# Norm tiles, engine orders, norm statistics and the score sign in a two-layer decoder

## The chip, the cores and the metric

The kernel runs on one core of a Trainium2 chip. The metric is the time of one execution in microseconds (us), as the device measures it; lower is better. The kernel before took 2627.57 us (median of three runs, 2625.74 to 2631.69). Five engines work side by side: TensorE (PE in the profile, its weight loads PEld), VectorE (DVE), ScalarE (ACT), GpSimd (POOL) and SyncE (SP), whose queue starts the transfers.

## The reference, cut to what matters

The input is one sequence of 1024 positions by 1024 channels, in float32. Layer 0 is a causal convolution module and a gated FFN; then one set of keys and values is projected; layer 1 is sparse attention (compressed, selected and window branches, 16 heads) and a second FFN; a last RMSNorm ends it.

```python
def rmsnorm(x, g):
    return x * lax.rsqrt(jnp.mean(x * x, axis=-1, keepdims=True) + EPS) * g

def conformer_conv(x, ...):
    a, b = jnp.split(rmsnorm(x, norm_g) @ pw1_w + pw1_b, 2, axis=-1)
    h = depthwise_conv31(a * sigmoid(b)) + dw_b
    h = silu(layernorm(h, ln_g, ln_b))          # the channel norm
    return h @ pw2_w + pw2_b

h = x + conformer_conv(x, ...)
h = h + swiglu_ffn(h, ...)                      # rmsnorm, 1024 -> 2 x 2816 -> 1024
kv = shared_kv(h, ...)                          # rmsnorm (kv_norm), projection
h = h + nsa_attention(h, ...)                   # rmsnorm (b_norm), 16 heads, softmax(s - slope * dist)
h = h + swiglu_ffn(h, ...)
out = rmsnorm(h, final_norm)
```

## The kernel before, in words

Everything is held with channels on the partitions: a half of the sequence (512 positions, c = 0 or 1) is eight tiles of 128 x 512, k = 0 to 7. A float32 product is made of three TensorE matmuls on a high and a low part: `split` (L172) writes the high part yh on ScalarE (L177) and then the low part yl = y - yh on VectorE or GpSimd (L179); `wload` (L142) does the same for a weight tile (wh L158, wl L160), and `mm3` (L123, L137) issues wh*yh, wh*yl and wl*yh for each k. One weight tile against eight k is 24 matmuls.

A norm has these steps. `sumsq` (L182) squares a tile on ScalarE (L189) and adds it to an accumulator on VectorE or GpSimd (L190). `rstd_parts` (L192) makes the sum over channels: four small matmuls (L201), each with 128 columns of the accumulator as the stationary operand and one column of ones. They are put into a list, `sides`, and `mm3` issues one of them behind each of its own matmuls. Ten small VectorE operations make the reciprocal root (`rsqrt`, L252 to L262), a VectorE operation lays it on a diagonal (`diagonal`, L213), and a matmul with ones spreads it over the partitions (`spread`, L220). Then `norm_y` (L265) writes each normed tile (L272, VectorE) and splits it. While `roomy` holds (the first 760 us or so), every normed tile whose low part is made on VectorE is put into PSUM, in a pool of eight buffers with one tag that also serves all matmul results and the convolution; otherwise it goes into a temporary in SBUF (tag "a", five buffers, four later). In the channel norm, `centre` (L378) sums the accumulator over channels (L382), subtracts the mean (L385) and squares; `normal` (L393) multiplies by the reciprocal root (L401), applies SiLU on ScalarE (L403; for c = 0 into PSUM) and splits.

The norms, by the order in which their tiles are used: n1 and n2, the first RMSNorm of the halves 0 and 1; n3, the channel norm of half 0; n4, the FFN norm of half 0; n5, the channel norm of half 1; n6, the key/value norm of half 0; n7, the FFN norm of half 1; n8, the key/value norm of half 1; n9 and n10, the second FFN norms of the halves 0 and 1; n11, the last norm of half 0. Behind n6 and n8 an attention norm uses the same reciprocal root, kept in SBUF (`kept`). n1, n2 and n4 to n11 use one accumulator; n3 hands its eight squares to the statistics one by one.

TensorE's order is the order in which the program issues its matmuls. `go(main, time)` runs generators of foreground work for a stated time of TensorE; `behind` interleaves a second generator at a rate: the convolution of a half (`conv`, `conv_tile`, L303: up to ten taps on ScalarE and GpSimd, L328 and L329, four on TensorE, L320, the rest on VectorE, L332), then `layernorm(1)` (L408), later the attention. The `yield` numbers in `layernorm` are the times that pass between its steps. The orders of VectorE, ScalarE and GpSimd are written by a planner from its own times of the operations; buffers are given out in that plan, too. `mark` remembers an instruction of an engine, and `later` adds an edge without a semaphore that puts an instruction behind the one marked.

In attention `scores` (L949) adds scaled scores and a distance term and takes the running maximum in one VectorE operation (L987), negates the maximum (L993, VectorE), and ScalarE takes the exponential with it as the bias (L995).

Of the kernel before, what the change touches and what calls it, by code (L numbers as in the profile page):

```python
# [20 lines left out]
F32 = mybir.dt.float32  # L21
# [6 lines left out]
KT = 8  # L28
NC = 2
T = 512  # L30
# [7 lines left out]
NEG = -1e30  # L38
# [60 lines left out]
PRINT = 0  # L99
YB = 16  # L100


class Net:
# [69 lines left out]
    def split(self, src, lo="dve"):  # L173
# [3 lines left out]
        nc.scalar.activation(yh, src, AF.Copy)  # L177
# [4 lines left out]
    def sumsq(self, c, k, src, eng, pool=None):  # L182
# [107 lines left out]


# [102 lines left out]
    def normal(self, c):  # L394
# [4 lines left out]
        y = []  # L399
        for j in range(KT):  # L400
            self.later(nc.vector.tensor_tensor(z[j], z[j], r, OP.mult))  # L401
            s = self.tmp("si") if c or j in LNP[c] else self.mm_ps()
            nc.scalar.activation(s, z[j], AF.Silu, bias=self.vec[:, V_LNB + j:V_LNB + j + 1],  # L403
                                 scale=self.vec[:, V_LNG + j:V_LNG + j + 1])
            y.append(self.split(s, "pool" if j in LNP[c] else "dve"))
        if c == 0:
            self.mark(self.last)
        self.yln[c] = y  # L408

    def layernorm(self, c):  # L410

        yield 4.0
        self.centre(c)
        yield 10.0
        self.sides.extend(self.rstd_parts([self.acc[c]]))
        yield 6.0
        while self.sides:
            yield 1.0
        self.rstd_spread(c, True)
# [408 lines left out]
    def q_tile(self, j, c):  # L828
# [73 lines left out]
    def bias_base(self):  # L902
# [3 lines left out]
        for (c0, w, step, off) in ((0, S, 1, 896), (BT_WIN, 640, 1, 512),  # L906
                                   (BT_CMP, 119, 16, 896 - (LC - 1))):
            nc.gpsimd.iota(b[:, c0:c0 + w], pattern=[[step, w]], base=-off,
                           channel_multiplier=-1, allow_small_or_imprecise_dtypes=True)
            nc.gpsimd.affine_select(out=b[:, c0:c0 + w], in_=b[:, c0:c0 + w],  # L910
                                    pattern=[[-step, w]], compare_op=OP.is_ge, fill=NEG,
                                    base=off, channel_multiplier=1)
        nc.gpsimd.affine_select(out=b[:, BT_WIN:BT_WIN + 640], in_=b[:, BT_WIN:BT_WIN + 640],
                                pattern=[[1, 640]], compare_op=OP.is_ge, fill=NEG,
# [34 lines left out]
    def scores(self, out, K, q, g, head, i, win):  # L949


        nc = self.nc
# [589 lines left out]
```

## Time and profile before

| | |
|---|---|
| median of three runs | 2627.57 us (2625.74 to 2631.69) |
| the profiled execution | 2629.18 us |
| its span, first to last instruction | 2627.5 us |
| PE busy | 2512.0 us, 96% |
| DVE busy | 1765.8 us, 67% |
| POOL busy | 1469.2 us, 56% |
| ACT busy | 1291.6 us, 49% |
| mean granted TensorE clock | 0.981 |

A share is an average over stages with different limits. An engine's idle time costs something only where the instruction that it waits for ends last, so the waits of TensorE are what is to be read, each at its place in the timeline. The granted clock is a share of full speed: 1.00 is 2.4 GHz, 0.50 is 1.2 GHz.

### The profile page before, as it was taken

What the parts mean: (1) busy time and instruction counts of PE and PEld (TensorE: products, weight loads), DVE (VectorE), ACT (ScalarE), POOL (GpSimd) and SP (SyncE); (2) the same over time, 40 slices, a digit from 0 to 9 for tenths busy, and PEclk for the clock granted to TensorE, in tenths of its full rate; (3) what the DMA queues carried; (4) which work ended last, traced back from release to release, by engine and by line L of the source; (5) the groups of instructions that cost most, each with busy time, mean ns of one, the idle gap of its engine ahead of it and who ended that gap; (6) DMA issues with size and microseconds to landing.
All of it is one profiled execution on the core that took longest, in us unless ns stands there. A gap on an engine that the chain in (4) does not pass through costs nothing. (4 is left out here: it accounts for less than half of the span.)

```text
span 2627.5 us, 37191 instructions
## 1 busy us (share of the span) xinstructions
PE 2512.0 (96%) x12946; PEld 2083.5 (79%) x12946; DVE 1765.8 (67%) x3652; ACT 1291.6 (49%) x2517; POOL 1469.2 (56%) x1156
## 2 busy tenths in 40 slices
PE   8898899999799999999999999999999999899997
PEld 6676788888677878887878788888888887698986
DVE  6995788677774556665556566667666655777775
ACT  6555554444534554555543355555555543334444
POOL 8794889666543554555543354535445433566664
PEclk9999899999899999999999999999999999999999
DMA  4222223232446222322355531213212124143332
GB/s 163 72 73 66 80 81 97 88 93 92 152 146 190 87 89 62 112 86 82 90 161 167 190 101 45 81 44 108 70 53 74 54 78 158 58 129 97 97 95 75
DMA packets 111212, 258.29 MB, mean 98 GB/s; under 512 B 17265, under 2 KB 28848, under 8 KB 111024
## 3 DMA queue, kind: packets, MB, share of 16 engines
q1 hardware_dynamic: 111024, 255.91, 31.0%
q8 instruction: 102, 1.67, 0.3%
q14 instruction: 86, 0.70, 0.1%
HBM read 226.37 MB, written 29.42 MB: 97 GB/s over the span
## 5 line engine op out<-in xcount | busy, mean ns | idle before, releaser
L160 POOL TENSOR_TENSOR wl<-wr,wh 128x1024 fp32r<-128x1024 f32 (+2 forms) x396 | 740.6, 1872 | 661.1 <-ACT wh L158 625.1
L137 PE MATMUL mm<-yh,wh 128*128 128x512 f32 x1424 | 595.4, 418 | 31.7 <-DVE yl L179 30.4
L137 PE MATMUL mm<-yl,wh 128*128 128x512 f32 x1424 | 567.6, 399 | 5.0 <-DVE yl L179 5.0
L137 PE MATMUL mm<-yh,wl 128*128 128x512 f32 x1424 | 566.2, 398 | 1.8 <-POOL wl L160 1.8
L158 ACT ACTIVATE wh<-wr 128x1024 fp32r<-128x1024 f32 (+2 forms) x396 | 332.5, 840 | 426.3 <-PE mm L137 287.1
L137 PE MATMUL mm<-gh,wh 128*128 128x512 f32 x1360 | 439.4, 404 | 1.8 <-ACT gh L592 1.4
L137 PEld LDWEIGHTS mm<-yh,wh 128*128 128x128 f32 x1424 | 272.1, 191 | 86.3 <-DVE yl L179 32.1
L137 PEld LDWEIGHTS mm<-yh,wl 128*128 128x128 f32 x1424 | 271.3, 191 | 63.5 <-POOL wl L160 2.2
L137 PEld LDWEIGHTS mm<-yl,wh 128*128 128x128 f32 x1424 | 272.6, 191 | 49.5 <-DVE yl L179 6.2
L1030 DVE TENSOR_TENSOR pl<-pt,ph 128x512 fp32r<-128x512 f32 (+3 forms) x320 | 206.4, 646 | 149.6 <-ACT ph L1029 148.7
L137 PEld LDWEIGHTS mm<-gh,wh 128*128 128x128 f32 x1360 | 243.3, 189 | 48.8 <-issue 3.5
L137 PE MATMUL mm<-gh,wl 128*128 128x512 f32 x680 | 270.0, 397 | 3.7 <-POOL wl L160 3.7
L1029 ACT ACTIVATE ph<-pt 128x512 fp32r<-128x512 f32 (+3 forms) x320 | 178.7, 559 | 177.6 <-PE pt L1026 175.2
L1000 POOL TENSOR_SCALAR PS<-PS,sm,gates 128x31 f32<-128x31 f32 (+9 forms) x256 | 154.7, 615 | 191.4 <-DVE sm L997 164.6
L332 DVE SCALAR_TENSOR_TENSOR mm<-u,vec,mm 128x512 f32<-128x512 f32 x306 | 225.6, 752 | 8.0 <-PE mm L320 1.8
L995 ACT ACTIVATE PS<-PS,mx 128x31 f32<-128x31 f32 (+9 forms) x256 | 139.5, 546 | 115.6 <-DVE mx L993 115.3
L329 POOL TENSOR_TENSOR zb<-zb,cv 128x512 f32<-128x512 f32 x132 | 178.8, 1355 | 14.4 <-ACT zb L314 8.8
L1000 POOL TENSOR_SCALAR PW<-PW,sm,gates 128x640 f32<-128x640 f32 (+4 forms) x128 | 96.2, 752 | 155.1 <-DVE sm L997 131.8
L606 DVE TENSOR_TENSOR h<-mm,h 128x512 f32<-128x512 f32 x184 | 124.7, 684 | 81.7 <-PE mm L137 81.3
L137 PEld LDWEIGHTS mm<-gh,wl 128*128 128x128 f32 x680 | 128.0, 188 | 37.7 <-POOL wl L160 7.5
L995 ACT ACTIVATE PW<-PW,mx 128x640 f32<-128x640 f32 (+4 forms) x128 | 88.8, 694 | 101.2 <-DVE mx L993 100.5
L507 PE MATMUL mm<-y,wh 128*128 128x256 f32 x1008 | 133.8, 286 | 2.3 <-DVE wh L492 1.9
(243 smaller groups left out, 4814.4 us busy)
## 6 DMA issues: line engine op xcount, KB each, us to landing
wr<-in_fin_dram SPq DMA_DIRECT2D x176, 512.0 KB, 3.3
wr<-in_fout_dram SPq DMA_DIRECT2D x128, 256.0 KB, 2.7
wr<-in_pw_dram SPq DMA_DIRECT2D x46, 512.0 KB, 3.3
wr<-in_fout_dram SPq DMA_DIRECT2D x64, 192.0 KB, 2.4
wr<-in_wq_dram SPq DMA_DIRECT2D x16, 512.0 KB, 4.0
qd<-q SPq DMA_DIRECT2D x32, 256.0 KB, 2.2
qt<-qd SPq DMA_DIRECT2D x32, 256.0 KB, 2.8
wr<-in_wo_dram SPq DMA_DIRECT2D x16, 512.0 KB, 3.7
```

The costliest lines, as they stand in the source:

```text
L137: nc.tensor.matmul(ps, x[:, a, :], y_, start=start and a + b == 0, stop=stop and a == n - 1 and b == 2)
L158: nc.scalar.activation(wh[:, :kt, :cols], wr[:, :kt, :cols], AF.Copy)
L160: e.tensor_tensor(wl[:, :kt, :cols], wr[:, :kt, :cols], wh[:, :kt, :cols].bitcast(F32), OP.subtract)
L329: nc.gpsimd.tensor_tensor(zb, zb, t, OP.add)
L332: later(nc.vector.scalar_tensor_tensor(ps, u[:, w:w + T], dw(w), ps, OP.mult, OP.add))
L507: nc.tensor.matmul(ps, u[:, a], v, start=a + b == 0, stop=a == n - 1 and b == 2)
L606: self.nc.vector.tensor_tensor(h, ps, h, OP.add)
L995: nc.scalar.activation(P[:, p0:p0 + pn], P[:, p0:p0 + pn], AF.Exp, bias=mx[:, e:e + 1], accum_out=sm[:, e:e + 1])
L1000: nc.gpsimd.tensor_scalar(P[:, p0:p0 + pn], P[:, p0:p0 + pn], sm[:, e:e + 1], self.gates[:, i, gt:gt + 1], OP.mult, OP.mult)
L1029: nc.scalar.activation(ph[:rows, :width], pt[:rows, :width], AF.Copy)
L1030: nc.vector.tensor_tensor(pl[:rows, :width], pt[:rows, :width], ph[:rows, :width].bitcast(F32), OP.subtract)
```

## The change

Six things are changed. (1) In `norm_y`, while `roomy` holds, only even tiles go into PSUM; odd ones go into SBUF temporaries. (2) Edges without a semaphore fix orders: in `norm_y`, tile k is written behind the second-last low part made on VectorE before it; in `normal`, VectorE's multiplication stands behind the third-last low part, and ScalarE's SiLU behind the second-last high part; the attention norm's tiles stand behind the last low part of the key/value norm; for half 0, ScalarE's part of the later convolution stands behind the channel norm's last high part. (3) The last square of a norm is not added to the accumulator: it goes to the statistics as a second tile, so there are eight small matmuls in the place of four. (4) That last square takes a buffer of tag "rs" (two buffers, shared with the diagonal and the kept reciprocal root). (5) `layernorm(1)` has other times between its steps. (6) The score's sign is turned: queries, distances and the mask value have the other sign, a running minimum takes the place of the maximum, the exponential has scale -1, and the negation is gone.

```diff
+AHEAD = 2
...
-        nc.scalar.activation(yh, src, AF.Copy)
+        self.first = nc.scalar.activation(yh, src, AF.Copy)
...
             nc.scalar.activation(self.acc[c], src, AF.Square)
-        else:
+        elif k < KT - 1:
             sq = pool.tile([128, T], F32, name="sq", tag="b") if pool else self.tmp("sq")
             nc.scalar.activation(sq, src, AF.Square)
             eng.tensor_tensor(self.acc[c], self.acc[c], sq, OP.add)
+        else:
+
+            sq = self.sq[c] = self.cp.tile([128, T], F32, name="sl", tag="rs", bufs=2)
+            nc.scalar.activation(sq, src, AF.Square)
...
-        self.sides.extend(self.rstd_parts(tiles or [self.acc[c]]))
+        self.sides.extend(self.rstd_parts(tiles or [self.acc[c], self.sq[c]]))
...
-        y = []
+        y, low = [], []
         for k in range(KT):
-            t = self.mm_ps() if self.roomy and k not in pool else self.tmp("yt")
-            nc.vector.scalar_tensor_tensor(t, self.h[c][k], self.vec[:, vcol + k:vcol + k + 1],
-                                           r, OP.mult, OP.mult)
+            t = self.mm_ps() if self.roomy and k % 2 == 0 and k not in pool else self.tmp("yt")
+            ins = nc.vector.scalar_tensor_tensor(
+                t, self.h[c][k], self.vec[:, vcol + k:vcol + k + 1], r, OP.mult, OP.mult)
+            if kept:
+                self.later(ins)
+            if len(low) >= AHEAD:
+                self.order(ins, low[-AHEAD])
             y.append(split(t, k) if split else self.split(t, "pool" if k in pool else "dve"))
+            if not split and k not in pool:
+                low.append(self.last)
...
+    def order(self, ins, old):
+
+        self.tc.add_manual_dep(ins.ins, old.ins.name, mybir.DependencyInfo(
+            mybir.DependencyClass.NoSync, mybir.DependencyReason.DATA))
...
-            self.later(nc.vector.tensor_tensor(z[j], z[j], r, OP.mult))
+            ins = nc.vector.tensor_tensor(z[j], z[j], r, OP.mult)
+            self.later(ins)
+            if len(low) > AHEAD:
+                self.order(ins, low[-1 - AHEAD])
             s = self.tmp("si") if c or j in LNP[c] else self.mm_ps()
...
+            if len(high) >= AHEAD:
+                self.order(ins, high[-AHEAD])
             y.append(self.split(s, "pool" if j in LNP[c] else "dve"))
+            high.append(self.first)
+            if j not in LNP[c]:
+                low.append(self.last)
         if c == 0:
             self.mark(self.last)
+            self.mark(self.first)
...
     def layernorm(self, c):
 
-        yield 4.0
+        yield 10.0
         self.centre(c)
-        yield 10.0
-        self.sides.extend(self.rstd_parts([self.acc[c]]))
-        yield 6.0
+        yield 16.0
+        self.sides.extend(self.rstd_parts([self.acc[c], self.sq[c]]))
+        yield 1.0
         while self.sides:
             yield 1.0
+        yield 14.0
         self.rstd_spread(c, True)
...
-            f = DH ** -0.5 / SLOPE[g * HG + j]
+            f = -DH ** -0.5 / SLOPE[g * HG + j]
...
-                    SLOPE[head], init, OP.add, OP.max, mx[:, col:col + 1])
+                    SLOPE[head], init, OP.add, OP.min, mx[:, col:col + 1])
...
-        nc.vector.tensor_scalar(mx[:, :ns], mx[:, :ns], -1.0, None, OP.mult)
         for e, (br, p0, pn, b0) in enumerate(segs):
-            nc.scalar.activation(P[:, p0:p0 + pn], P[:, p0:p0 + pn], AF.Exp,
+            nc.scalar.activation(P[:, p0:p0 + pn], P[:, p0:p0 + pn], AF.Exp, scale=-1.0,
...
         self.y[0] = self.norm_y(0, V_KVN)
+        self.mark(self.last)
...
         self.y[1] = self.norm_y(1, V_KVN)
+        self.mark(self.last)
```

## Rows read from the trace of the kernel before

**Rows 1.** The page's first part: busy time, share of the span, instructions.
```profile
PE 2512.0 (96%) x12946; PEld 2083.5 (79%) x12946; DVE 1765.8 (67%) x3652; ACT 1291.6 (49%) x2517; POOL 1469.2 (56%) x1156
```

**Rows 2.** Stretches round eight waits: length; busy PE, PEld, DVE, ACT, POOL; PEclk; DMA.
```profile
103.50:116.10 12.60, 6.18 (x16) 4.82 (x16) 12.60 (x20) 6.82 (x12) 11.92 (x8) 0.60 0.31 107
232.70:245.70 13.00, 2.77 (x8) 2.15 (x8) 7.28 (x13) 11.89 (x20) 11.29 (x9) 0.61 0.14 42
293.80:304.10 10.30, 7.43 (x23) 6.13 (x24) 6.84 (x13) 3.83 (x6) 7.95 (x4) 0.67 0.31 102
307.20:317.70 10.50, 5.24 (x13) 4.14 (x14) 10.50 (x17) 7.18 (x13) 7.43 (x6) 0.67 0.16 51
698.60:710.10 11.50, 6.55 (x19) 5.51 (x20) 7.78 (x17) 4.21 (x5) 7.22 (x3) 0.70 0.50 160
714.60:727.10 12.50, 4.01 (x10) 3.14 (x11) 12.50 (x20) 5.53 (x10) 2.35 (x1) 0.59 0.30 106
1376.20:1386.10 9.90, 7.22 (x22) 6.02 (x23) 5.45 (x13) 2.81 (x4) 7.21 (x3) 0.66 0.59 189
2242.90:2249.70 6.80, 3.41 (x8) 2.69 (x9) 6.53 (x8) 3.19 (x7) 2.35 (x1) 0.75 0.23 77
```

**Rows 3.** The busy ends of two of these stretches, TensorE alone: length, busy, PEclk.
```profile
109.90:116.10 6.20, 6.17 (x15) 0.50 0.01 3
...
296.60:304.10 7.50, 7.43 (x23) 0.54 0.43 140
```

**Rows 4.** Timeline of TensorE, small matmuls among large ones: start, length, instruction.
```profile
209.36 0.40 PE L137 MATMUL mm<-yh,wh 128*128 128x512 f32 x1
209.59 0.28 PE L201 MATMUL mm<-ones,sq 128*128 128x1 f32 x2
...
210.04 0.28 PE L201 MATMUL mm<-ones,sq 128*128 128x1 f32 x2
```

**Rows 5.** Timeline: last sum before n3's centre, and the centre's matmul.
```profile
196.65 0.68 DVE L343 TENSOR_TENSOR acc<-acc,z 128x512 f32<-128x512 f32 x1
...
201.66 1.02 PE L382 MATMUL mm<-acc,ones 128*128 128x512 f32 x2
```

**Rows 6.** Busy time in two convolution stretches, columns as in Rows 2.
```profile
100.00:200.00 100.00, 91.87 (x357) 68.44 (x356) 96.35 (x133) 54.92 (x88) 83.59 (x53) 0.95 0.23 75
...
400.00:470.00 70.00, 70.00 (x306) 57.05 (x305) 58.38 (x80) 35.73 (x52) 62.65 (x41) 1.00 0.32 100
```

**Rows 7.** Low parts on VectorE by source: shapes, count | busy us, mean ns | idle.
```profile
L179 DVE TENSOR_TENSOR yl<-yt,yh 128x512 fp32r<-128x512 f32 x30 | 32.3, 1109 | 0.1
...
L179 DVE TENSOR_TENSOR yl<-mm,yh 128x512 fp32r<-128x512 f32 x30 | 19.1, 681 | 5.7 <-ACT yh L177 5.7
```

**Rows 8.** Timeline of ScalarE in n3 and at the first weight behind it.
```profile
231.62 1.47 ACT L403 ACTIVATE mm<-z,vec 128x512 f32<-128x512 f32 x2
...
241.61 2.98 ACT L177 ACTIVATE yh<-mm 128x512 fp32r<-128x512 f32 x6
...
252.56 1.06 ACT L158 ACTIVATE wh<-wr 128x1024 fp32r<-128x1024 f32 x1 [7.97 <-PE mm L137]
```

**Rows 9.** Timeline of VectorE: last accumulator sums of n4 and n6.
```profile
293.80 2.82 DVE L190 TENSOR_TENSOR acc<-acc,sq 128x512 f32<-128x512 f32 x1 [2.18 <-POOL acc L190]
...
699.26 4.23 DVE L190 TENSOR_TENSOR acc<-acc,sq 128x512 f32<-128x512 f32 x3
```

**Rows 10.** Timeline: last sum before n5's centre, and the centre's matmul.
```profile
456.39 2.83 DVE L343 TENSOR_TENSOR acc<-acc,z 128x512 f32<-128x512 f32 x1
...
463.14 1.02 PE L382 MATMUL mm<-acc,ones 128*128 128x512 f32 x2
```

**Rows 11.** Timeline of VectorE in n6: tiles of the attention norm.
```profile
717.83 3.34 DVE L272 SCALAR_TENSOR_TENSOR yt<-h,vec,rs 128x512 f32<-128x512 f32 x4
```

**Rows 12.** The score's negation on VectorE: shapes, count | busy us, mean ns | idle.
```profile
L993 DVE TENSOR_SCALAR mx<-mx 128x1 f32<-128x1 f32 (+1 forms) x256 | 81.0, 319 | 3.5
```

**Rows 13.** Waits of TensorE in attention: us in total, times, longest.
```profile
PE po L1051 <- DVE pl L1030: 3.4, 9, 0.7
```

More of the change, by code (lines that the diff above doesn't have):

```diff
@@ L37 @@
 EPS = 1e-6
-NEG = -1e30
+FAR = 1e30
 LC = 32
@@ L398, in normal @@
         r = self.rs[c] if c else self.rp[c]
-        y = []
+        y, low, high = [], [], []
         for j in range(KT):
-            self.later(nc.vector.tensor_tensor(z[j], z[j], r, OP.mult))
+            ins = nc.vector.tensor_tensor(z[j], z[j], r, OP.mult)
+            self.later(ins)
+            if len(low) > AHEAD:
+                self.order(ins, low[-1 - AHEAD])
             s = self.tmp("si") if c or j in LNP[c] else self.mm_ps()
-            nc.scalar.activation(s, z[j], AF.Silu, bias=self.vec[:, V_LNB + j:V_LNB + j + 1],
-                                 scale=self.vec[:, V_LNG + j:V_LNG + j + 1])
+            ins = nc.scalar.activation(s, z[j], AF.Silu,
+                                       bias=self.vec[:, V_LNB + j:V_LNB + j + 1],
+                                       scale=self.vec[:, V_LNG + j:V_LNG + j + 1])
+            if len(high) >= AHEAD:
+                self.order(ins, high[-AHEAD])
             y.append(self.split(s, "pool" if j in LNP[c] else "dve"))
+            high.append(self.first)
+            if j not in LNP[c]:
+                low.append(self.last)
         if c == 0:
             self.mark(self.last)
+            self.mark(self.first)
         self.yln[c] = y
     def layernorm(self, c):
-        yield 4.0
+        yield 10.0
         self.centre(c)
-        yield 10.0
-        self.sides.extend(self.rstd_parts([self.acc[c]]))
-        yield 6.0
+        yield 16.0
+        self.sides.extend(self.rstd_parts([self.acc[c], self.sq[c]]))
+        yield 1.0
         while self.sides:
             yield 1.0
+        yield 14.0
         self.rstd_spread(c, True)
@@ L907, in bias_base @@
                                    (BT_CMP, 119, 16, 896 - (LC - 1))):
-            nc.gpsimd.iota(b[:, c0:c0 + w], pattern=[[step, w]], base=-off,
-                           channel_multiplier=-1, allow_small_or_imprecise_dtypes=True)
+            nc.gpsimd.iota(b[:, c0:c0 + w], pattern=[[-step, w]], base=off,
+                           channel_multiplier=1, allow_small_or_imprecise_dtypes=True)
             nc.gpsimd.affine_select(out=b[:, c0:c0 + w], in_=b[:, c0:c0 + w],
-                                    pattern=[[-step, w]], compare_op=OP.is_ge, fill=NEG,
+                                    pattern=[[-step, w]], compare_op=OP.is_ge, fill=FAR,
                                     base=off, channel_multiplier=1)
         nc.gpsimd.affine_select(out=b[:, BT_WIN:BT_WIN + 640], in_=b[:, BT_WIN:BT_WIN + 640],
-                                pattern=[[1, 640]], compare_op=OP.is_ge, fill=NEG,
+                                pattern=[[1, 640]], compare_op=OP.is_ge, fill=FAR,
                                 base=-1, channel_multiplier=-1)
@@ L984, in scores @@
                     spare += 1
-                init = mx[:, prev[e]:prev[e] + 1] if e in prev else -3.0e38
+                init = mx[:, prev[e]:prev[e] + 1] if e in prev else 3.0e38
                 prev[e] = col
@@ L1261, in run @@
         self.acc, self.rs, self.rp, self.y, self.yln, self.yo = {}, {}, {}, {}, {}, {}
+        self.sq = {}
         self.u, self.z, self.G = {0: {}, 1: {}}, {0: {}, 1: {}}, {0: {}, 1: {}}
```

## The prediction

> **What bounds the kernel now.** The first part of the page comes first: TensorE is busy for 2512.0 of 2627.5 us and no other engine for more than 67% [rows 1]. So the time is TensorE's work plus its waits, some 115 us, and the next view is who made it wait, and where. Eight stretches stand out, each with one long wait and then a busy end [rows 2]; all lie in norms. Read a row so: length minus busy PE is the wait, 12.60 - 6.18 = 6.4 us in the first. What follows runs at half clock: the stretch behind that wait has a granted clock of 0.50 and another 0.54 [rows 3], so about half of its busy time is lost as well (0.47 where the clock is 0.54). Lost in all:
>
> - n2, 103.5: 6.4 + 3.1 = 9.5 us
> - n3, 232.7: 10.2 + 1.4 = 11.6
> - n4 statistics, 293.8: 2.9 + 3.5 = 6.4
> - n4 tiles, 307.2: 5.3 + 2.6 = 7.9
> - n6 statistics, 698.6: 5.0 + 3.3 = 8.2
> - n6 tiles, 714.6: 8.5 + 2.0 = 10.5
> - n8 statistics, 1376.2: 2.7 + 3.4 = 6.1
> - n10 tiles, 2242.9: 3.4 + 1.7 = 5.1
>
> That is 65.3 us. In n2, n3, n4's tiles and n6's tiles I read the wait as one for a buffer: counting the matmuls since each spread by the program's order, TensorE stands at a foreground matmul that needs nothing of the norm (in n6 the next tile of pw2), only one of the eight PSUM buffers, and normed tiles or SiLU results hold them. VectorE is busy through the whole of 714.6 to 727.1 (12.50 of 12.50) in the order that the planner gave it, many tiles first and low parts later. In the statistics the wait is for the last accumulator sum: 2.82 us in n4, and 4.23 us for three in n6 [rows 9], where one such sum in the clear takes 0.7 (the last sum of a convolution, 0.68 [rows 5], has the same shape).
>
> **The change part by part.**
>
> *Even tiles only, and the fixed order.* Tile k+2 is written behind low part k, so one normed tile in PSUM and one in SBUF live at a time: buffers stay free and the foreground goes on.
>
> n6 tiles: seven tiles of pw2 are left as cover, far more than the norm takes. All of 10.5 can go; I take 10 (7 to 10.5). The attention norm's four early tiles, 3.34 us of VectorE [rows 11], move behind the last low part. They were waiting for space afterwards anyway, so I cost the move at nothing; without that cover it is their 3.34 us.
>
> n4 tiles: the second half of a pw1 tile, 24 matmuls or 5.5 us, becomes cover. Then the FFN needs the tiles one by one. I take 6.5 of 7.9 (3 to 7.9).
>
> n3: here the order does it, since its SiLU results stay in PSUM. SiLU takes 1.47 us for two and high parts 2.98 us for six [rows 8], together 0.73 + 0.50 = 1.2 us a tile, 9.8 us for eight. From 231.62 that ends at 241.4 us; one weight conversion on ScalarE (1.06) and a low part (0.7) put the last tile at 243.2 and, three matmuls on, TensorE's end of that weight tile at 243.9. In the trace it gives this weight's place back at about 252.5 us (ScalarE's L158 starts at 252.56, having waited for PE [rows 8]). The difference is 8.6; I take 8.5 (5 to 10). The convolution's ScalarE work, pushed behind the last high part, keeps GpSimd waiting for some 10 us; what that costs is below.
>
> n2: 9.5 us are lost here, but little of that comes through. VectorE is at 96.35 of 100 us between 100 and 200 [rows 6], nearly all convolution; its last sum ends at 197.3 and the centre's matmul, in TensorE's fixed order, stands at 201.66 [rows 5]. So TensorE can come at most 4.3 us earlier, the rest becomes a wait there and perhaps another half-clock end. Inside this stage are also the added small matmuls of n1 and n2 (1.8, below). I take +1.5 (-2 to 4).
>
> n10 has its tiles in SBUF as before; only the order moves. Its wait is for a low part, and one place earlier is worth about two operations, 1.4 us. I take 1.5 (-1 to 4).
>
> *The low parts from SBUF.* From PSUM the 30 low parts take 681 ns on average, from SBUF 1109, with the same shape [rows 7]; the excess is 0.43 us. Eleven move to SBUF (four in n2, three in n4, four in n6; n4's tiles 1 and 4 were there), 4.7 us of VectorE. In n4 and n6 that lies in the slack; in n2 it is 1.7 us, and it is in the 1.5. The Trainium skill has a rule that speaks against this edit (SBUF — State Buffer, section "SBUF: two separate sides"): a VectorE instruction with two SBUF inputs and a GpSimd instruction that reads SBUF exclude each other for the whole instruction. The trace agrees, with the 1109 against 681 ns. By that rule alone n2 would end at the second rival below, whose price comes from rows.
>
> *The last square unadded.* Ten norms (all but n3) get four more small matmuls. Between large ones a large one alone takes 209.59 - 209.36 = 0.23 us, and with a small one 210.04 - 209.59 = 0.45 [rows 4], so a small one costs 0.22: 0.9 us a norm, 9.0 in all. What goes is one sum per norm, on the path only where TensorE waits for it.
>
> - n4: the sum waited 2.18 us for GpSimd's sum before it, and itself took 2.82 [rows 9]. That earlier sum is done when TensorE arrives, so up to 6.4 - 0.9 = 5.5 are free; but GpSimd is busy there, and I take 3.5 (0 to 5.5).
> - n6: without the third of the 4.23 us [rows 9] the second ends at about 699.26 + 2 x 0.68 = 700.6, while TensorE comes at 698.6. A wait of 2 us is left. I take 4 of 8.2 - 0.9 (0 to 7.3).
> - n8: the wait is the last sum alone; 6.1 - 0.9, I take 5 (0 to 5.2).
> - n1 and n2 are in n2's figure; n5, n7, n9, n10 and n11 did not wait: -4.5.
>
> The new "rs" buffer is free in time: a kept root and one of square or diagonal fill two places, and the square is read before the diagonal is written. I cost it at nothing; if it weren't, the square would wait for a spread, some 5 us in one norm.
>
> *More time in the channel norm.* n5's centre stands at 463.14 us, its last sum ends at 459.2 [rows 10]: 3.9 us of slack. Six more units at the background's rate of 0.7 add 8.6, so 12.5. TensorE comes some 20 us earlier by n2 to n4, while the convolution behind it runs on VectorE and GpSimd, GpSimd at 62.65 of 70 us [rows 6] and with n3's 10 us deferred. What they don't make up is a wait. I take -4 (0 to -10). The other steps of n5 have the rest of the FFN as cover.
>
> *The score sign.* 256 negations go, 81.0 us of VectorE [rows 12], but TensorE waits in attention for little, 3.4 us for the low part of the probabilities being the largest [rows 13]. The minimum and the scaled exponential take the place of like operations. I take 2 (0 to 5).
>
> **Sum.** 1.5 + 8.5 + 3.5 + 6.5 - 4 + 4 + 10 + 5 + 1.5 - 4.5 + 2 = 34.0 us. From the profiled execution, 2629.2, that gives 2595.2; the median of the runs is 1.6 lower, so 2593.6, said as 2594. The low ends of all terms together make about zero, the high ends 55.
>
> **The rivals.**
>
> 1. *Everything comes through.* VectorE and GpSimd keep up, so the convolution gives nothing back: 65.3 less 9.0 for small matmuls and 3.0 for what n3 can't give, plus 3.4 in attention, 57 us: 2571. For it: GpSimd idles 10% even in its fullest stretch. Against it: VectorE's 96 of 100 us before n3 [rows 6].
>
> 2. *The convolution is the bound up to 464 us.* TensorE meets its last sums at both centre matmuls and what n2, n3 and n4 gained (20) is lost there, 16 more than the 4 already charged: 18 us, 2610. For it: slacks of 4.3 and 3.9 us [rows 5, 10], and low parts that meet GpSimd [rows 7]. Against it: the longer times before n5's centre.
>
> 3. *The buffers stay short.* The change doesn't do what it says, since other temporaries and the convolution fill the freed places: only statistics and attention change, 3.5 + 4 + 5 - 4.5 - 1.8 + 2 = 8 us: 2619. Against it: at most two normed tiles live at a time.
>
> 4. *Slower: the order makes VectorE stand.* Each low part waits for its high part, and VectorE can't go on past it. Where ScalarE converts a weight first, 1.06 us [rows 8], each tile can lose that; 8.5 us a norm. At the five norms with little cover (n2, n3, n4, n9, n10) that is 42 us against the 34: 2636. It decides from 0.85 us lost a tile. Against it: the next tile's multiplication covers most of a high part, and ScalarE is busy for 7.18 of 10.50 us in n4 [rows 2].
>
> **How the numbers follow.** A measurement of this kernel can tell 0.2%, 5.3 us. Forecast 0.55 (2582 to 2606 by itself), rival 1 0.12, rival 2 0.18, rival 3 0.08, rival 4 0.07. Half of rival 3 and 0.02 of rival 4 lie within 0.2%: same 0.06, slower 0.05, faster 0.89. The range 2568 to 2617 leaves out a third of rival 1, most of rival 3, rival 4 and the far end of rival 2, some 0.19.
>
> **What would show it.** Right: no wait over 1 us for a low part in n2, n4 and n6, TensorE at clock 1.00 there; in ten norms four small matmuls on a last square behind four on the accumulator; n3's wait split into short ones; L993 gone. The forecast is wrong if a new wait of over 5 us stands at L382, or if waits for low parts stay above 15 us in total.

## The result, and the profile after

The changed kernel takes 2598.67 us (median of 4 runs, 2594.19 to 2600.18), the kernel before 2626.65 (4 runs beside it): ratio 0.9889, 95% interval 0.9868 to 0.9910, 28.0 us less. Forecast were 2594.0 in a range of 2568 to 2617. The total is right to 4.7 us; its terms are not, and several errors cancel. Every version has its own line numbers: L138 and L180 of the changed kernel are L137 and L179 of the kernel before.

The first part of the page after, against [rows 1]: busy time, share of the span (2598.5 us), instructions.

```profile
PE 2508.5 (97%) x13026; PEld 2087.5 (80%) x13026; DVE 1709.2 (66%) x3388; ACT 1300.3 (50%) x2517; POOL 1468.2 (57%) x1154
```

VectorE has 264 instructions fewer: 256 negations and 8 of the ten last sums (two of its sums of before were GpSimd's). TensorE has 80 records more, two for each of 40 small matmuls. TensorE's idle time is 2598.5 - 2508.5 = 90.0 us against 115.5, which is 25.5 of the 29.0 us between the two profiled spans.

The same windows as in [rows 2], laid round the places where TensorE waits or waited in the changed kernel; columns as there.

```profile
107.50:130.00 22.50, 9.31 (x16) 3.94 (x15) 22.32 (x34) 11.40 (x20) 11.30 (x9) 0.64 0.21 70
240.00:253.00 13.00, 7.40 (x25) 5.61 (x24) 10.68 (x18) 12.94 (x22) 4.18 (x3) 0.74 0.15 50
292.00:306.00 14.00, 13.96 (x68) 11.18 (x67) 4.14 (x13) 5.54 (x7) 13.33 (x9) 1.00 0.28 93
306.00:318.00 12.00, 12.00 (x54) 9.81 (x54) 11.40 (x18) 9.82 (x17) 7.12 (x5) 1.00 0.19 68
495.00:507.00 12.00, 5.23 (x25) 4.23 (x24) 11.58 (x24) 5.22 (x10) 8.74 (x8) 0.69 0.14 45
699.00:711.00 12.00, 9.20 (x35) 7.50 (x34) 6.38 (x15) 2.63 (x3) 6.23 (x3) 0.72 0.54 188
712.00:728.00 16.00, 16.00 (x71) 12.87 (x70) 13.35 (x19) 7.89 (x12) 2.43 (x2) 1.00 0.14 50
746.50:760.00 13.50, 7.42 (x22) 5.55 (x21) 10.70 (x10) 6.62 (x11) 11.14 (x9) 0.75 0.68 232
1361.00:1372.00 11.00, 11.00 (x56) 8.93 (x55) 3.87 (x14) 4.71 (x6) 6.57 (x3) 1.00 0.73 233
2216.00:2226.00 10.00, 7.66 (x25) 5.46 (x25) 4.96 (x6) 4.62 (x6) 3.73 (x2) 0.83 0.18 59
```

Four of the eight waits are gone, with the clock at 1.00: n4's statistics (third line) and tiles (fourth), n6's tiles (seventh), n8 (ninth). n3 (second) and n6's statistics (sixth) wait about half as long as before. n10 (tenth) has a longest wait of 1.9 us in place of 3.4. The first, fifth and eighth lines are places that lost. TensorE's waits over the whole span say for what: us in total, times, longest.

```profile
PE mm L336 <- ACT dgw L335: 10.3, 6, 5.4
PE mm L138 <- DVE yl L180: 9.6, 5, 5.6
PE mm L534 <- ACT y L479: 8.4, 3, 3.5
PE mm L336 <- DVE yl L180: 7.8, 1, 7.8
PE mm L138 <- POOL wl L161: 7.7, 9, 2.3
PE mm L138 <- DVE h L455: 6.1, 1, 6.1
```

L336 is a tap of the convolution (at 116 and 125 us), L534 a matmul of the first seven products (498 to 504 us), L138 behind L455 the first weight tile of the KV stage (753 us).

TensorE's foreground matmuls (L138, L534, L1374 and their counterparts) stand in a written order that no version changes, and their 9672 records have the same order of names in every trace. So the start of the same matmul in two traces tells where time came from. The table gives this lag, start in a version minus start in the kernel before, in us (negative is earlier). The versions are those of the next section.

| start before | what lies just ahead | changed | sign_only | no_order | early_centre | sel | best2 |
|---|---|---|---|---|---|---|---|
| 70.7 | n1 | 2.0 | 0.0 | 2.9 | 2.5 | 0.4 | 0.3 |
| 202.1 | n2, first convolution | 8.0 | 0.0 | 5.3 | 8.7 | 0.2 | 0.3 |
| 280.0 | n3 | 3.9 | 1.2 | 2.0 | 4.7 | -2.9 | -2.6 |
| 329.5 | n4 | -9.1 | -0.6 | -10.4 | -8.4 | -16.0 | -15.1 |
| 443.5 | FFN of half 0, first product | -6.4 | -0.6 | -10.4 | -5.6 | -16.0 | -15.1 |
| 507.2 | n5's centre, first seven products | 4.1 | -0.6 | -2.2 | -5.6 | -10.1 | -11.1 |
| 607.1 | rest of that FFN | -0.7 | -2.7 | -6.9 | -8.9 | -12.2 | -13.5 |
| 734.6 | n6 | -10.7 | -4.0 | -17.6 | -16.2 | -22.8 | -27.6 |
| 784.2 | KV weights | -3.2 | -4.0 | -17.9 | -8.8 | -15.1 | -27.9 |
| 818.2 | rest of the KV stage | -9.0 | -4.2 | -20.6 | -14.6 | -20.9 | -30.6 |
| 829.9 | n7's small matmuls | -8.0 | -4.2 | -19.6 | -13.6 | -20.9 | -29.6 |
| 1359.3 | first attention | -12.7 | -8.9 | -24.3 | -18.4 | -25.6 | -34.3 |
| 1413.5 | n8 | -18.0 | -11.0 | -29.5 | -23.6 | -30.8 | -39.5 |
| 1523.1 | KV of half 1, n9 | -18.4 | -11.0 | -29.5 | -27.3 | -28.6 | -43.9 |
| 2163.5 | second attention | -27.1 | -20.1 | -38.1 | -36.1 | -37.7 | -53.0 |
| 2260.0 | n10 | -27.4 | -19.5 | -40.9 | -36.7 | -39.4 | -55.7 |
| 2599.9 | last FFN, n11 | -28.9 | -20.9 | -41.9 | -36.9 | -38.2 | -58.3 |

So the change loses 8.0 us up to the first convolution's end, gains 4.0 in n3 and 13.0 in n4, loses 8.4 up to 607, gains 8.3 up to 818, loses 1.0 at n7's small matmuls, gains 4.7 and 8.7 in the two attentions, 5.3 in n8, and 0.4, 0.3 and 1.5 at n9, n10 and the end.

A lag is one execution against one other. The changed kernel, old_times and early_centre differ only in n5, and yet lie at 8.0, 7.2 and 8.7 at 202; n2_psum and both_old, alike up to n5 too, at 3.9 and 5.8. sign_only is 4.2 us ahead at 818, ahead of the first negation (859 us), and gains 2.1 at n8, where it edits nothing. A step of 2 us in one column shows little by itself; one that comes back in every column shows more.

### The profile page after: what moved, and what is told of

Same layout as the page of the kernel before. It is cut to its first block, busy times and chain, and to the rows that moved or that the text cites. A ratio compares the mean times of both kernels' runs of the same rounds, so it can differ in the third digit from the quotient of the medians.

```text
span 2598.5 us, 37137 instructions
## 1 busy us (share of the span) xinstructions
PE 2508.5 (97%) x13026; PEld 2087.5 (80%) x13026; DVE 1709.2 (66%) x3388; ACT 1300.3 (50%) x2517; POOL 1468.2 (57%) x1154
## 4 chain that ended last, share of the span: by engine, by line
PE 74%; DVE 12%; POOL 4%; DMA 4%; issue 4%; ACT 2%; SPq 0%; DVEq 0%; ACTq 0%; POOLq 0%
PE mm L138 51%; PE po L1078 6%; PE sc L1003 5%; PE mm L534 5%; PE pt L1053 5%; POOL wl L161 2%; POOL zb L345 1%; DVE yl L180 1%; DVE yt L277 1%; DMA wr<-in_fout_dram 1%; DVE mm L348 1%; DVE acc L191 1%; DVE wh L519 1%; DMA wr<-in_fin_dram 1%; ACT wh L159 1%
## 5 line engine op out<-in xcount | busy, mean ns | idle before, releaser
L138 PE MATMUL mm<-yh,wh 128*128 128x512 f32 x1424 | 594.1, 417 | 12.9 <-DVE h L455 6.1
L138 PE MATMUL mm<-yl,wh 128*128 128x512 f32 x1424 | 566.0, 397 | 4.3 <-DVE yl L180 4.0
L138 PE MATMUL mm<-yh,wl 128*128 128x512 f32 x1424 | 565.8, 397 | 3.9 <-POOL wl L161 3.9
L138 PE MATMUL mm<-gh,wh 128*128 128x512 f32 x1360 | 439.4, 403 | 1.7 <-ACT gh L619 1.3
L138 PEld LDWEIGHTS mm<-yh,wh 128*128 128x128 f32 x1424 | 271.2, 190 | 65.4 <-issue 23.9
L138 PEld LDWEIGHTS mm<-yh,wl 128*128 128x128 f32 x1424 | 270.4, 190 | 65.5 <-POOL wl L161 4.8
L138 PEld LDWEIGHTS mm<-yl,wh 128*128 128x128 f32 x1424 | 271.9, 191 | 50.4 <-DVE yl L180 6.3
L138 PEld LDWEIGHTS mm<-gh,wh 128*128 128x128 f32 x1360 | 242.6, 188 | 48.9 <-issue 4.0
L138 PE MATMUL mm<-gh,wl 128*128 128x512 f32 x680 | 269.8, 397 | 3.8 <-POOL wl L161 3.8
L138 PEld LDWEIGHTS mm<-gh,wl 128*128 128x128 f32 x680 | 127.6, 188 | 37.3 <-POOL wl L161 7.2
L534 PE MATMUL mm<-y,wh 128*128 128x256 f32 x1008 | 135.4, 289 | 0.9 <-DVE wh L519 0.7
L138 PE MATMUL mm<-yP,wh 128*128 128x512 f32 (+1 forms) x416 | 134.7, 402 | 0.0
```

The costliest lines, as they stand in the source:

```text
L138: nc.tensor.matmul(ps, x[:, a, :], y_, start=start and a + b == 0, stop=stop and a == n - 1 and b == 2)
L534: nc.tensor.matmul(ps, u[:, a], v, start=a + b == 0, stop=a == n - 1 and b == 2)
```

## The experiments

Ratios are to the kernel before, run on the same chip beside each.

**1. The sign alone** (sign_only). The kernel before with the last part of the change:

```diff
-                    SLOPE[head], init, OP.add, OP.max, mx[:, col:col + 1])
+                    SLOPE[head], init, OP.add, OP.min, mx[:, col:col + 1])
-        nc.vector.tensor_scalar(mx[:, :ns], mx[:, :ns], -1.0, None, OP.mult)
```

> The kernel before with the score sign turned and nothing else (256 negations on VectorE gone). Theory from the two traces: TensorE gained 3.4 us over the first attention and 8 to 9 over the second, so about 11 us faster than before, 2613 to 2617, with the waits of the probabilities' transposes for GpSimd gone. Rival, the forecast's own term: 2 us (0 to 5), so 2622 to 2627; the rest of the gain in those stretches then comes from the norms' edits by a better position of the background.

Measured 2611.23 us, ratio 0.9939 (0.9927 to 0.9952): 16 us, over half of the whole change's 28. That is more than theory (11) and rival (2) had; the forecast's term (2, at most 5) falls. The table puts 4.7 us into 830 to 1359 and 9.1 into 1523 to 2164, and every version gains nearly the same there (4.7 or 4.8, and 8.6 to 9.1). The two profiled executions lie 21.0 us apart; the 4.2 of them ahead of 818 are not put down to the sign. The waits don't show as much as the attentions gain. Waits of TensorE in the second attention, of the kernel before and then of this one:

```profile
PE po L1051 <- DVE pl L1030: 2.8, 8, 0.7
PE po L1051 <- ACT ph L1029: 1.9, 2, 1.3
```

```profile
PE po L1050 <- DVE pl L1029: 0.4, 2, 0.3
```

The same stretch by windows, from the same matmul to the same matmul, before and this one, columns as in [rows 2]:

```profile
1523.06:2163.46 640.40, 635.17 (x3389) 532.17 (x3388) 422.43 (x1260) 357.37 (x739) 300.35 (x279) 1.00 0.22 68
```

```profile
1512.04:2143.36 631.32, 630.81 (x3389) 532.98 (x3388) 392.08 (x1132) 362.58 (x740) 301.54 (x279) 1.00 0.22 69
```

The same matmuls take 640.4 and 631.3 us. Idle time explains 5.2 - 0.5 = 4.7 of the 9.1; the other 4.4 is busy time that shrank from 635.17 to 630.81 at a clock of 1.00 in both. I read it as waiting counted as busy, since most of the 9.1 lies at attention's own matmuls: from start to next start, idle time included, the 256 po<-ph matmuls take 49.5 us before and 45.1 here, po<-pl 47.0 and 45.7, the transposes 71.9 and 70.6, the mm<-yh,wl of that stretch 84.2 and 82.6; the other kinds agree within 0.3. In the first attention the transposes of PS fall from 22.6 to 19.2. Whether TensorE was held by VectorE's 30 us of load or by the 0.32 us that each negation put between maximum and exponential was not told apart.

**2. The old times in n5** (old_times), and **3. its first time alone** (early_centre):

```diff
 # early_centre; old_times also: 16.0 -> 10.0, 1.0 -> 6.0, 14.0 gone
-        yield 10.0
+        yield 4.0
         self.centre(c)
```

> The changed kernel with the old times in the channel norm of half 1 (4, 10, 6 and 2 units). Theory: the longer times put VectorE's centring and sums (466 to 482 us) into the additions that prepare the first seven-product weights and inputs, and TensorE's waits for them at 498 to 504 us cost some 7 us; with the old times the centre comes at 465.6 - 6 / 0.7 = 457.0, behind the convolution's last sum (454.8), those waits go, and the run takes 2590 to 2594. Rival, the forecast's term: the convolution isn't ready, the centre's matmul waits, and the run is 2 to 8 us slower than the changed kernel, 2601 to 2607.

> The changed kernel with the first time of the channel norm of half 1 back at 4 units (the centre's matmul 8.6 us earlier), the other longer times kept. Theory: the first time alone did the harm, since it moves VectorE's centring and sums from 457 to 471 us, where VectorE is idle, to 466 to 482 us, where the first seven-product inputs are made; so the waits at 498 to 504 us go: 2589 to 2594, as with all the old times (2591.3). Rival: the later statistics and spread do it, and the run stays at 2596 to 2600.

Measured 2591.31 us, 0.9868 (0.9854 to 0.9881), and 2594.2, 0.9872 (0.9856 to 0.9888): 5.5 and 4.5 us below the changed kernel by the ratios, whose intervals overlap with its own; by the table early_centre is 9.7 us ahead of the changed kernel at 507 and 8.0 at the end (old_times 10.6 and 8.4). The first time alone is enough. Changed kernel, last sum of the convolution, the centre's matmul and VectorE's first work behind it, and then TensorE's waits from 480 to 520 us:

```profile
454.10 0.69 DVE L359 TENSOR_TENSOR acc<-acc,z 128x512 f32<-128x512 f32 x1
...
465.63 1.02 PE L398 MATMUL mm<-acc,ones 128*128 128x512 f32 x2
466.69 4.87 DVE L401 SCALAR_TENSOR_TENSOR z<-mm,z 128x512 f32<-128x512 f32 x8 [9.03 <-PE mm L398]
...
480.60 1.22 DVE L191 TENSOR_TENSOR acc<-acc,sq 128x512 f32<-128x512 f32 x1
```

```profile
PE mm L534 <- ACT y L479: 5.9, 2, 3.5
PE mm L534 <- DVE y L480: 0.7, 1, 0.7
```

VectorE stands 9.03 us until the centre's matmul comes, with its sum ready since 454.8, and then centres, sums and makes the first seven-product inputs (L297, L480) at once. In early_centre it does the first from 458.64 to 470.1, in the gap, and no wait is left between 440 and 520:

```profile
458.64 4.87 DVE L401 SCALAR_TENSOR_TENSOR z<-mm,z 128x512 f32<-128x512 f32 x8 [0.17 <-PE mm L398]
463.43 6.68 DVE L191 TENSOR_TENSOR acc<-acc,sq 128x512 f32<-128x512 f32 x6
```

**4. The second norm as before** (n2_psum):

```diff
-        self.y[1] = self.norm_y(1, V_ANORM)
+        self.y[1] = self.norm_y(1, V_ANORM, step=1)   # all tiles in PSUM, no order
```

> The changed kernel with the second norm (half 1, in front of pw1) as before: all eight normed tiles in PSUM, no fixed order. Theory: the loss of 8 us in that stage comes from the four SBUF tiles and the order, which put VectorE's tiles behind convolution taps; so the waits of the convolution's matmuls at 116 and 125 us go, the wait at 104 to 110 comes back, and TensorE reaches the first channel norm's centre 5 to 8 us earlier than in the changed kernel: 2591 to 2595. Rival: VectorE and GpSimd are the bound of this stage whichever way the tiles are held, so the centre comes at the same time, and the run stays at 2597 to 2600.

Measured 2594.9 us, 0.9881 (0.9866 to 0.9896); the interval does not part it from the changed kernel. The trace does in that stage: at 202 us the lag is 3.9 instead of 8.0, a little less than the theory wanted. Tiles and taps of VectorE in the changed kernel:

```profile
95.52 0.75 DVE L277 SCALAR_TENSOR_TENSOR mm<-h,vec,mm 128x512 f32<-128x512 f32 x1
...
104.78 6.29 DVE L348 SCALAR_TENSOR_TENSOR mm<-u,vec,mm 128x512 f32<-128x512 f32 x8
110.97 0.74 DVE L277 SCALAR_TENSOR_TENSOR yt<-h,vec,mm 128x512 f32<-128x512 f32 x1
```

and the first tiles in n2_psum, from 94.85:

```profile
94.85 2.07 DVE L277 SCALAR_TENSOR_TENSOR mm<-h,vec,mm 128x512 f32<-128x512 f32 x3
```

The second tile, in SBUF, comes 15 us behind the first, after 17 taps of the convolution; the norm's last low part ends at 127 us instead of 118, and a tap on TensorE (L336) waits 7.8 us for a low part. n2_psum waits at L138 in its place, 6.4 us, as the kernel before. It undoes place and order together; two later versions part them. no_order, with SBUF tiles and no order, has the same 15 us (first and second tile):

```profile
96.45 0.75 DVE L277 SCALAR_TENSOR_TENSOR mm<-h,vec,mm 128x512 f32<-128x512 f32 x1
...
111.91 0.74 DVE L277 SCALAR_TENSOR_TENSOR yt<-h,vec,mm 128x512 f32<-128x512 f32 x1
```

and all_psum, with the order and no SBUF tile, writes both at once:

```profile
96.47 1.41 DVE L277 SCALAR_TENSOR_TENSOR mm<-h,vec,mm 128x512 f32<-128x512 f32 x2
```

So it is the place in SBUF that puts the second tile off.

**5. The sum back** (sums_back): the last square is added again, four small matmuls a norm.

```diff
-        elif k < KT - 1:
+        else:
...
-        self.sides.extend(self.rstd_parts(tiles or [self.acc[c], self.sq[c]]))
+        self.sides.extend(self.rstd_parts(tiles or [self.acc[c]]))
```

> The changed kernel with the last square added to the accumulator again and four small matmuls a norm. Theory by the traces: n4 loses about 3 and n8 5.5 us of gains, n6 nothing, and 40 small matmuls of 0.22 us, 9, come back: within 2 us of the changed kernel, 2597 to 2602. Rival, the forecast's terms (3.5 + 4 + 5 gained, 6.3 paid): 6 us slower than the changed kernel, 2603 to 2607. A third: the sum was hidden everywhere but in n8, then the edit costs: 3 to 4 us faster, 2594 to 2596.

Measured 2602.73 us, 0.9903 (0.9889 to 0.9916): just between theory and rival, 3.7 us above the changed kernel by the ratio, 2.2 by the traces, neither of them clear of it. By its lags the added sum gains 4.4 us in n1 and n2 (3.6 against 8.0 at 202) and 1.0 at n7, and loses 5.0 in n4, 1.0 in n6 and 2.9 in n8 (that stretch gains 2.4 in sums_back, 5.3 in the changed kernel). The edit pays in n4 and n8 and loses in n1 and n2; the 1.0 in n6 is within what two executions differ by.

**6. No fixed order** (no_order; the edges behind marked instructions stay), and **7. all tiles in PSUM, in order** (all_psum):

```diff
-AHEAD = 2
+AHEAD = 99                                               # no_order
...
-            t = self.mm_ps() if self.roomy and k % 2 == 0 and k not in pool else self.tmp("yt")
+            t = self.mm_ps() if self.roomy and k not in pool else self.tmp("yt")   # all_psum
```

> The changed kernel without the fixed order between low parts and later tiles (VectorE) and between high parts and later SiLUs (ScalarE); even tiles alone in PSUM stay. Theory: with four of eight tiles in PSUM and four SBUF temporaries the places alone keep buffers free in the FFN norm of half 0 and the KV norm, so 16 us of gains there stay; only the first channel norm, whose SiLU results are all in PSUM, falls back to its long wait (10.2 us before, 5.6 in the changed kernel): 2600 to 2606. Rival: the order does it, and the waits of all three norms come back, 20 us: 2614 to 2620.

> The changed kernel with all normed tiles in PSUM again, in the fixed order. Theory: the order alone lets at most two or three tiles live at a time, so no wait comes back in the FFN norm of half 0 and the KV norm, and in the second norm low parts read PSUM: 2594 to 2599. Rival: the even tiles do it, and 16 us of waits come back: 2610 to 2616. With the run without the order this tells which of the two edits carries the gain, or that either does.

Measured 2584.0 us, 0.9835 (0.9818 to 0.9851), and 2600.27, 0.9899 (0.9884 to 0.9914). Without the order the kernel is 14 us faster than with it, with no overlap of the intervals; neither theory nor rival of mine had that sign. The second run lies just above its theory, as fast as the changed kernel within the intervals. With the order and all tiles in PSUM, waits come back in n4 (4.0 us, 5.3 in the kernel before) and n6 (8.5 before):

```profile
PE mm L138 <- DVE yl L180: 5.8, 1, 5.8
```

no_order has neither wait. So the even tiles free the buffers, the order alone does it in part, and beside them the order costs. The largest piece of that cost lies behind n6. VectorE of the changed kernel (L277 with rs: the attention norm's tiles; L455: the sum that reads a pw2 tile out of PSUM), then a weight conversion of the KV stage on ScalarE and what follows it on VectorE:

```profile
715.22 0.75 DVE L277 SCALAR_TENSOR_TENSOR mm<-h,vec,mm 128x512 f32<-128x512 f32 x1
715.87 0.74 DVE L277 SCALAR_TENSOR_TENSOR yt<-h,vec,mm 128x512 f32<-128x512 f32 x1
716.53 2.20 DVE L191 TENSOR_TENSOR acc<-acc,sq 128x512 f32<-128x512 f32 x1
718.65 0.68 DVE L180 TENSOR_TENSOR yl<-mm,yh 128x512 fp32r<-128x512 f32 x1
...
726.98 0.69 DVE L180 TENSOR_TENSOR yl<-yt,yh 128x512 fp32r<-128x512 f32 x1
727.58 4.87 DVE L277 SCALAR_TENSOR_TENSOR yt<-h,vec,rs 128x512 f32<-128x512 f32 x4
732.38 0.73 DVE L455 SCALAR_TENSOR_TENSOR h<-mm,vec,h 128x512 f32<-128x512 f32 x1
```

```profile
745.56 1.06 ACT L159 ACTIVATE wh<-wr 128x1024 fp32r<-128x1024 f32 x1 [4.43 <-DMA wr<-in_wkv_dram]
...
747.17 2.42 DVE L191 TENSOR_TENSOR acc<-acc,sq 128x512 f32<-128x512 f32 x1 [2.88 <-ACT sq L190]
...
752.38 0.74 DVE L455 SCALAR_TENSOR_TENSOR h<-mm,vec,h 128x512 f32<-128x512 f32 x1
```

The same in no_order:

```profile
712.89 0.74 DVE L277 SCALAR_TENSOR_TENSOR yt<-h,vec,mm 128x512 f32<-128x512 f32 x1
...
719.92 0.74 DVE L455 SCALAR_TENSOR_TENSOR h<-mm,vec,h 128x512 f32<-128x512 f32 x1
...
740.34 0.75 DVE L455 SCALAR_TENSOR_TENSOR h<-mm,vec,h 128x512 f32<-128x512 f32 x1
```

Four places in PSUM and four in SBUF hold all eight tiles, so without the order VectorE writes them in one run (708.28 to 713.6) and ScalarE's high parts follow about 0.65 us apart; in order most follow 1.25 us apart, and a sum of 2.20 us stands between the second tile and the first low part. That does not make the norm late: from its start (ScalarE's copy of the spread, at 713.91 and 706.98, 6.9 us apart) to its last low part it takes 13.8 us in order and 15.8 without. What comes late is VectorE's other work. The next pw2 tile is read out at 732.38, behind the attention norm's four tiles, instead of 719.92, among the low parts: 5.5 us later in itself. The read-outs behind it follow one another by way of ScalarE's squares and VectorE's sums, and a square stands behind a weight conversion that waits 4.43 us for its load, so the delay stays: the last read-out lies at 752.38 instead of 740.34, 5.1 us later in itself. TensorE waits for it, 6.1 us up to 753; in no_order it waits 1.0 there, for a weight.

Between 734.6 and 784.2 the changed kernel gives back 7.5 us, no_order nothing; up to 818 the changed kernel wins 5.8 again and no_order 2.7, so this place is worth 4.7 of the 13 us between the two traces. By 734.6 the changed kernel is 6.9 us behind already (2.7 at 202, 1.3 at 329.5, 4.0 at 443.5, 6.3 at 507.2); between 375 and 405 it waits 1.9 us for GpSimd's low parts of a weight and no_order does not. That the order makes these is not shown.

**8. n3 without its mark** (n3_no_mark), on no_order:

```diff
-            self.mark(self.first)
```

> The kernel without the fixed order (2584.0 us) and, in the first channel norm, also without the mark that keeps ScalarE's convolution work behind the last high part; this norm is then as in the kernel before. Theory: the mark, not the order of high parts and SiLUs, shortened TensorE's wait there from 10.2 to 5.7 us, so the wait of 10 us comes back: 2586 to 2592. Rival: the wait is shorter for another reason (the background stands elsewhere), and it stays near 5.7: 2582 to 2586.

Measured 2590.24 us, 0.9851 (0.9837 to 0.9866), some 4 us slower than no_order by the ratios, whose intervals overlap; between 202 and 280 its lag rises by 0.5 us where that of no_order falls by 3.3. ScalarE and TensorE's wait in it, and ScalarE's next weight:

```profile
232.32 3.35 ACT L344 ACTIVATE cv<-u,vec 128x512 f32<-128x512 f32 x5
235.58 1.47 ACT L422 ACTIVATE mm<-z,vec 128x512 f32<-128x512 f32 x2
...
257.03 1.06 ACT L159 ACTIVATE wh<-wr 128x1024 fp32r<-128x1024 f32 x1 [8.47 <-PE mm L138]
```

```profile
PE mm L138 <- DVE yl L180: 10.2, 1, 10.2
```

The wait of 10.2 us is back (5.7 in no_order, 5.6 in the changed kernel). Nine copies for the convolution lie ahead of the SiLUs and among them; the mark puts them behind the last high part, and that is what shortened n3, not the order of SiLUs and high parts.

**9. Both losing parts undone** (both_old: experiments 2 and 4 together), and **10. that, with the last square unadded in n4, n6 and n8 only** (sel):

```diff
-        elif k < KT - 1:
+        elif k < KT - 1 or (c, self.nsum[c]) not in UNADDED:
+            self.sq[c] = None
```

> The changed kernel with the old times in the channel norm of half 1 and with the second norm as before (all PSUM, no order): the two parts of the change that lost, undone together. Theory: they lie in different stretches (70 to 210 us and 465 to 530 us) with TensorE busy between, so the gains of 7.4 and 3.8 us add: 2585 to 2590. Rival: TensorE 4 us earlier meets the last sum of the second convolution at the centre (2.2 us of margin by the traces), and the gains don't add: 2590 to 2593.

> As the run before, and the last square left unadded only in the three norms that waited for the last sum (FFN half 0, KV half 0, KV half 1); in the other seven it is added again, without the four small matmuls. Theory: 7 x 0.9 = 6.2 us of small matmuls go, the added sums are hidden: 2579 to 2584. Rival: in those seven the sum is on the path for as long as the small matmuls were, and nothing changes: 2585 to 2590.

Measured 2593.93 us, 0.9873 (0.9852 to 0.9893), and 2585.14, 0.9840 (0.9816 to 0.9863). The first lies above theory and rival, the second in its rival's range; the four runs of sel lie 13 us apart (2577.56 to 2590.94), and the traced one is the slowest. The gains of 2 and 4 don't add. Not the centre is in the way, as the rival had it, but n5's statistics 16 us behind it, which come too early with the old time of 10 units. TensorE waits there for the accumulator, in both_old:

```profile
PE mm L206 <- DVE acc L191: 2.9, 1, 2.9
```

(2.5 in sel), the granted clock of the 16 us behind is 0.70, and the lag of both_old goes from -8.4 at 470 to 0.1 at 490. best2 below, with 12 units and TensorE as early as in sel, does not wait there. In sel n1 and n2 then cost nothing (0.2 at 202), so small matmuls (4) and tiles (4) together make up the stage's 8 us.

**11. What the runs point to** (best), and **12. its mend** (best2): no order, the times of n5 at 5, 12, 1 and 8, the last sum added again in n1 and n2; best2 takes n2's tiles in PSUM, and 14 for the 8.

```diff
-AHEAD = 2
+AHEAD = 99
...
-        yield 10.0
+        yield 5.0
         self.centre(c)
-        yield 16.0
+        yield 12.0
...
-        self.y[1] = self.norm_y(1, V_ANORM)
+        self.y[1] = self.norm_y(1, V_ANORM, step=1)      # best2 only
```

> The kernel without the fixed order (2584.0 us), with shorter times in the channel norm of half 1 (5, 12, 1 and 8 units for 10, 16, 1 and 14), and with the last square added again in the first two norms only. Theory: the waits at 493 to 502 us go (6.5 us, as in the run with the old times), and the first two norms' eight small matmuls and what they put off in the convolution go (4 to 5.6 us by the run that unadds three norms only): 2571 to 2576. Rival: TensorE, so much earlier, meets the convolution's last sums at the centre, as in the run with both parts undone, and only half of it stays: 2577 to 2582.

> The run before (2584.5 us), with the second norm's eight tiles all in PSUM, and the last time of the channel norm of half 1 back at 14 units. Theory: the second norm's stage ends 6.5 us earlier (TensorE then reaches the first channel norm as early as in the kernel before, as in the run that unadds three norms only), and the spread's wait of 3.5 us at 495 us, which the short time made, goes: 2572 to 2578. Rival: TensorE's earlier arrival meets the second convolution's last sum at the centre or its statistics' sum, and half of it is given back: 2579 to 2584.

Measured 2584.5 us, 0.9826 (0.9811 to 0.9840), so neither the forecast 2571 to 2576 nor the rival's 2577 to 2582: TensorE waits 10.4 us at 154 us for a convolution input and 3.5 at 495 us for the diagonal, which 8 units leave too little time. best2 takes 2574.16 us (2571.11 to 2575.66), 0.9803 (0.9790 to 0.9817), in the forecast range: 51.6 us below the kernel before, and below the changed kernel with no overlap. Only the first half of its theory holds: at 202 its lag is 0.3 and that of best 6.7. The wait for the diagonal went, but 443 to 507 still costs 4.0 us (4.4 in best), with 2.0 us of waits for the first seven-product inputs in its place. Luck helped instead: the stretch from 1413 to 1523, at which no edit aims, gains 4.4 us (1.6 in best, 0.4 in the changed kernel), since TensorE's waits for the compressed keys there are 2.0 us and not 3.2 as in the changed kernel or 4.7 as before. Its page, first part (span 2569.1 us):

```profile
PE 2496.6 (97%) x13010; PEld 2080.0 (81%) x13010; DVE 1698.7 (66%) x3388; ACT 1302.9 (51%) x2517; POOL 1468.6 (57%) x1156
```

## Why the prediction was right in the sum and wrong in its terms

Forecast and measured agree to 6 us in 34 by luck: the score sign gave 11.4 us more than its term, and n2, n3, n5 and n6 together some 24 less.

- **n2** (+1.5): -8.0. I saw that VectorE is full there, but put in only the longer low parts and 1.8 us of small matmuls, and bounded the loss at 2. The step that failed is "one normed tile in PSUM and one in SBUF live at a time: buffers stay free": beside the convolution an SBUF tile queues behind taps, tiles live longer, and TensorE stands at L336 [rows 2, 6]. The extra statistics cost 4.4, not 1.8.
- **n3** (8.5) **and n4** (3.5 + 6.5): 18.5 forecast, 17.1 measured, but not as split: n3 gave 4.0, below its range, and n4 13.0. In n3 a wait of 5.6 us stays, and what shortened it was the mark, which I had costed as a burden on GpSimd, not the order of SiLUs and high parts. n4's waits are gone as said; its last square was worth 5.0 by sums_back.
- **n5** (-4): -8.4 from 330 to 607. TensorE came only 6 us earlier by 443, not 20, the convolution's sum was ready 10.8 us before the centre, and I looked for the loss before it; 10.5 us of loss came behind it, from work that had lain in a gap of VectorE. "The other steps of n5 have the rest of the FFN as cover" failed: the first seven products need VectorE first. Nearest to the mechanism I named are 2.7 us lost from 330 to 443, with a wait for GpSimd's weights.
- **n6** (4 + 10): 10.0 up to 735, 8.3 up to 818. The tiles' wait went as forecast. The statistics' did not: 2.8 us of wait remain at 702 in place of 5.0, two weight waits of 2.3 and 1.2 us stand ahead of it, and the granted clock there is 0.72 (sixth line of the windows above). "I cost the move at nothing" for the attention norm's tiles was wrong: with the order they delay L455, and by it the start of the KV stage.
- **n8** (5): 5.3, but sums_back gains 2.4 in that stretch without the edit and sign_only 2.1; the square left unadded is worth 2.9. **n10** (1.5): 0.3. The statistics elsewhere (-4.5): n7's four small matmuls cost 1.0 us, as forecast, in every column that has them and nothing in sign_only and sel. The other four were not read one by one.
- **Score sign** (2): 16 alone, 13.4 in the two attentions of the changed kernel. The step "TensorE waits in attention for little" read the list of waits [rows 13] as all there is. By the matched windows nearly half of the second attention's gain stood as busy time.
- **Rival 4**, the order making VectorE stand, got 0.07 for its whole price. The order does cost, 14 us instead of 42, hidden under the even tiles' gain; but what is seen behind n6 is other work put off, not low parts held up by weight conversions.
- **The prediction's own signs** speak against it. The waits for low parts behind the first layer's input sum up to 9.6 + 7.8 = 17.4 us, above its limit of 15; one of 7.8 us stands in n2, where the clock is 0.64 and not 1.00; n3's wait is one of 5.6 us, not short ones. No wait stands at the centre's matmul, and the negation is gone, as it said.
- The low parts from SBUF: 41 of them take 1020 ns on average in the changed kernel, 1049 in no_order:

```profile
L180 DVE TENSOR_TENSOR yl<-yt,yh 128x512 fp32r<-128x512 f32 x41 | 41.7, 1020 | 1.6 <-ACT yh L178 1.3
```

```profile
L180 DVE TENSOR_TENSOR yl<-yt,yh 128x512 fp32r<-128x512 f32 x41 | 42.0, 1049 | 0.9 <-ACT yh L178 0.9
```

  The mean hides two kinds. In the changed kernel 30 of the 41 take at most 0.69 us. The other 11, of 1.13 to 2.88 us, all begin while a GpSimd instruction runs and end 0.55 us after it ends. Of the 30 low parts from PSUM in the kernel before, 15 begin while a GpSimd instruction runs, and none takes over 0.69 us. So what the Trainium skill says of VectorE and GpSimd excluding each other (SBUF — State Buffer, section "SBUF: two separate sides") agrees with the trace. But no_order, the faster kernel, has the slower low parts: that price lay beside other work.

Open: why the added statistics of n1 and n2 cost 4.4 us and not 1.8 (they move the convolution's start, and TensorE's waits at L336 change with it), what the order costs ahead of n6, and what moves the waits for the compressed keys between 1413 and 1523.

## What to carry to other kernels

A bounded buffer count already limits how far ahead an engine runs. A hand-written order on top of it can make the ordered work itself quicker and still cost time, because it puts off the engine's other work: look at what TensorE waits for next, not only at the norm. Move work into a gap of its engine, not away from a wait that isn't there: look where that engine is idle before and after the move. And sum start-to-start distances of a saturated stretch, not its waits: TensorE at 99% busy (635.17 of 640.40 us) still had 9 us to give. Compare such lags over several versions: one trace against one other errs by up to 2 us a step here.

## What was not expected of the hardware

The records seem to count part of a short stall as busy time: the same 3389 records at the same granted clock of 1.00 had 635.17 and 630.81 us of busy TensorE, 4.4 us apart, with 128 negations less on VectorE between their inputs. And the time behind a wait of several us is again slow, as in [rows 3]: in the changed kernel the granted clock is 0.50, the lower level, from 116.3 to 120.0 and from 125.5 to 130.0, right behind waits of 7.8 and 5.4 us, while the stretches without a wait in the table of windows stand at 1.00. Not every wait does it: in best the 25 us round the wait of 3.5 us at 495 have a clock of 1.00.
